# Input projection of a hybrid attention block: three weight tiles over all tokens instead of six over half

## The chip, the cores and the metric

One core of a Trainium2 chip runs the whole program. The metric is the device time of one execution in microseconds; the median of three runs of the kernel before is 1149.23 us (1146.63 to 1149.85).

## The reference

`reference.py` is a two-layer hybrid diffusion backbone on 1024 latent tokens of 1024 channels, with 256 context tokens, all in float32. Only the start of the first (even) layer matters here:

```
shift, scale, gate = silu(c) @ ada_w + ada_b          # 1024 values each
h = layer_norm(x) * (1 + scale) + shift               # 1024 tokens x 1024 channels
z = h @ w_in                                          # split into q, k, v, gates, latent ranks, ...
```

The context tokens go through the same steps with a modulation of their own. After it come gated linear attention and latent attention, an output projection, and a second layer with a Fourier and a spatial gating branch.

## The kernel before

**Number format.** A product of two float32 matrices is made of three TensorE products (`mm3`, L144): each operand is split into a rounded part `hi` (a cast on ScalarE) and the remainder `lo` (a subtraction, mostly on VectorE), and hi x hi, hi x lo and lo x hi are summed in one PSUM bank. There are 8 banks of 128 x 512.

**The start.** `startup` (L275) makes `h` transposed, channels on partitions: for each of 8 channel tiles of 128 a `hi` and a `lo` of 128 x 1024 tokens. A token tile (128 tokens) is loaded and normalized by `load_norm` (L233): statistics on VectorE, three small steps on GpSimd, one activation on ScalarE. TensorE transposes it. Shift and scale of a channel tile come from `modulation` (L243): 512 KB of `ada_w` are loaded and reduced against silu(c) on VectorE, twice per channel tile (custom instruction, L248). So channels "arrive" one by one, with 1 MB each. A weight tile (`weight` in `startup`, L298) is 1024 channels x 128 outputs, 512 KB, rounded on ScalarE (L302), its low part on VectorE or, for two tiles, GpSimd (L305).

There are six weight tiles in `FIRST`: two of q, two of k, and two of latent ranks. The string `ORDER` (L271) sets by hand the order in which steps are written: m is a modulation pair, w a weight, r a channel tile of the first 512 tokens, x a token tile of the second 512, s a channel tile of the second 512, C the state and the context's loads.

The first four token tiles are transposed at once into all 8 banks (L359) and copied from there into `xnT` (L368); GpSimd applies the shift to each of them (L323), ScalarE rounds it (L328), VectorE takes the low part (L329). As each becomes ready, `products` (L342) multiplies it with all weight tiles that are there: six banks hold six tiles x 512 tokens. The second 512 tokens are transposed one channel tile at a time (`second`, L346) in the two other banks, with shift and scale on ScalarE. Then the six banks are evacuated, and `rest` (L398) multiplies the six tiles with the second 512 tokens.

**What follows.** `in_proj_a` (L459) weaves `rest` with the context's own start (`startup_ctx`, L409: 16 reductions, 16 transposes, roundings), in the proportion of the costs that the steps yield, and then projects the 256 context tokens with four of the same weight tiles (96 products of 256 columns). Weights of the two q tiles are given back inside `rest`. Most tiles of 4 KB per partition share one pool of 48 buffers: a load waits in SyncE's queue until a buffer is free.

**Who orders.** A compiler places the instructions of each engine in one fixed list, mostly in the order of the program, but an instruction whose inputs it expects early can be put ahead of others. `k.order(a, b)` (L126) adds a tie without a wait: a stands behind b in the list of their engine. Engines then run their lists strictly in order.

Of the kernel before, what the change touches and what calls it, by code (L numbers as in the profile page):

```python
# [82 lines left out]
class K:  # L83
# [60 lines left out]
    def mm3(self, out, lhs, rhs, start, stop):  # L144
        t = self.nc.tensor
        t.matmul(out, lhs[0], rhs[0], start=start, stop=False)  # L146
        t.matmul(out, lhs[0], rhs[1], start=False, stop=False)  # L147
        t.matmul(out, lhs[1], rhs[0], start=False, stop=stop)  # L148
# [94 lines left out]
def modulation(k, j, which, cB, name, queue, bufs=None):  # L243

    aw = k.b4(name="aw")
    queue.dma_start(aw, k.A["ada0"][which, j])
    o = k.sm.tile([P, 1], F32, tag=f"{name}{which}", name=name, bufs=bufs)
    k.nc.vector.tensor_tensor_reduce(out=aw, in0=aw, in1=cB, scale=1.0, scalar=k.ab[:, j, which:which + 1],  # L248
                                     op0=ALU.mult, op1=ALU.add, accum_out=o)
    return o  # L250
# [20 lines left out]
ORDER = "m w w r m w w r m w r m m x r x x x r m C s r s m s s r s s s s"  # L271
PLO, DVEV, REST_CONSTS = (2, 4), (2, 4), T_KR


def startup(k, context):  # L275
# [9 lines left out]
    xs = [load_norm(k, A["x"][i * P:(i + 1) * P, :]) for i in range(4)]  # L285

    nc.vector.tensor_scalar(out=k.ab[:, :, 1], in0=k.ab[:, :, 1], scalar1=1.0, scalar2=None, op0=ALU.add)
    tiles, ws, mods = FIRST, [], []
    h = ([], [])

# [7 lines left out]
    def weight():  # L298
        n = len(ws)
        raw, hi, lo = k.b4(F32, (P, KD, P), name="wraw"), k.b4(F32R, (P, KD, P), name="hi"), k.b4(F32R, (P, KD, P), name="lo")  # L300
        nc.sync.dma_start(raw, A["we"][tiles[n]])
        nc.scalar.copy(out=hi, in_=raw)  # L302
        ws.append((hi, lo))
        eng = nc.gpsimd if n in PLO else nc.vector
        eng.tensor_tensor(out=lo, in0=raw, in1=f32(hi), op=ALU.subtract)  # L305
        catch_up()
        for j in range(len(h[0])):
            products(n, j)

    def mod():  # L310
        j = len(mods)
        mods.append([])
        for w in range(2):
            mods[j].append(modulation(k, j, w, cB, f"mod{j}", nc.sync, 1))
            catch_up()

    def affine(out, in_, j):

        sh, sc = mods[j]
        if out is not in_:  # L320
            nc.scalar.activation(out=out, in_=in_, func=AF.Identity, scale=sc, bias=sh)
        else:
            nc.gpsimd.tensor_scalar(out=out, in0=in_, scalar1=sc, scalar2=sh, op0=ALU.mult, op1=ALU.add)  # L323

    def part(j, x, o):

        hi, lo = h[0][j][:, o:o + 512], h[1][j][:, o:o + 512]
        nc.scalar.copy(out=hi, in_=x)  # L328
        sub = lambda: nc.vector.tensor_tensor(out=lo, in0=x, in1=f32(hi), op=ALU.subtract)  # L329
        if o:  # L330
            later.append(sub)
            return
        sub()
        for t in range(len(ws) if acc else 0):
            products(t, j)

    def ready(j, x):
        for z in h:
            z.append(k.b4(F32R, name="h"))
        part(j, x, 0)  # L340

    def products(t, j):  # L342
        cnt[t] += 1
        k.mm3(acc[t], (ws[t][0][:, j, :], ws[t][1][:, j, :]), (h[0][j][:, :512], h[1][j][:, :512]), cnt[t] == 1, cnt[t] == KD)

    def second(j):  # L346

        ps = k.bank()
        for i in range(4):
            nc.tensor.transpose(ps[:, i * P:(i + 1) * P], xs[i][:, j * P:(j + 1) * P], k.ident)  # L350
        t = k.w2(name="x2")
        affine(t, ps, j)
        part(j, t, 512)

    cnt, acc = [0] * len(tiles), []
    mod()
    weight()
    ps = [k.bank() for _ in range(KD)]
    for i in range(4):  # L359
        for j in range(KD):  # L360
            nc.tensor.transpose(ps[j][:, i * P:(i + 1) * P], xs[i][:, j * P:(j + 1) * P], k.ident)
    x = k.w2(name="x2")
    affine(x, ps[0], 0)
    ready(0, x)
    xnT = [k.b4(F32, (P, 2, 512), name="xnT") for _ in range(KD // 2)]
    for j in range(1, KD):
# [1242 lines left out]
```

## Time and profile before

| | |
|---|---|
| median of three runs | 1149.23 us |
| profiled execution | 1150.0 us, of it span 1147.5 us |
| TensorE busy | 1091.7 us (95%) |
| VectorE, ScalarE, GpSimd busy | 739.0, 556.6, 260.1 us |
| mean granted TensorE clock | 0.985 of full |
| moved by DMA | 131.89 MB, 115 GB/s over the span |

Busy time is the sum of an engine's instructions. A busy TensorE is not one at its peak, since its matmuls overlap. The granted clock is 1.0 at 2.4 GHz and 0.5 at 1.2 GHz. A timeline row gives start, duration, engine, line, operation, output and inputs with their shapes, and the count of merged instructions; in brackets the idle time before it and what ended it. A windows row gives the busy time of every engine in one stretch.

### The profile page before, as it was taken

To read this page: it belongs to the slowest core of one execution; us is meant where nothing else is said; L and a number is where in the kernel's file an instruction comes from. 1 tells how busy PE (TensorE), PEld (TensorE's weight loads), DVE (VectorE), ACT (ScalarE), POOL (GpSimd) and SP (SyncE) were. 2 spreads that over 40 slices of the span, in tenths; PEclk is the share of its full clock that TensorE was granted. 3 is DMA by queue.
4 is the path that set the end of the run, shared out by engine and by line. 5 is a ranking of instruction groups with operands and counts; after the bars stand their busy time and mean duration, and the time that the engine had idled before them with its cause. 6 is when DMAs were issued, how large, how long until landed. Compare 5 with 4: busy or idle time off the path is not lost.

```text
span 1147.5 us, 14546 instructions
## 1 busy us (share of the span) xinstructions
PE 1091.7 (95%) x5288; PEld 864.4 (75%) x5288; DVE 739.0 (64%) x1256; ACT 556.6 (49%) x956; POOL 260.1 (23%) x260
## 2 busy tenths in 40 slices
PE   5889999899999999999999999999999999999997
PEld 3668778677777777767677666888788888888885
DVE  6867784756655675765778677788526533664544
ACT  6285755576553367857767778313422223332000
POOL 3520000000000023332424466343101000022111
PEclk8989999899999999999999999999999999999999
DMA  9635662333435752113202424323400311125111
GB/s 373 243 127 194 210 229 101 118 119 111 183 120 178 240 156 52 24 47 88 66 4 51 124 74 137 121 110 134 160 1 1 109 38 56 55 69 200 62 55 55
DMA packets 41752, 131.89 MB, mean 115 GB/s; under 512 B 5673, under 2 KB 7465, under 8 KB 41682
## 3 DMA queue, kind: packets, MB, share of 16 engines
q1 hardware_dynamic: 35578, 114.77, 30.5%
q0 software_dynamic: 3312, 10.26, 2.3%
q10 hardware_dynamic: 2792, 5.94, 1.3%
q8 instruction: 41, 0.67, 0.2%
q14 instruction: 29, 0.24, 0.1%
HBM read 98.37 MB, written 20.36 MB: 103 GB/s over the span
## 4 chain that ended last, share of the span: by engine, by line
PE 75%; DVE 8%; ACT 7%; issue 4%; POOL 3%; DMA 3%; SPq 1%; POOLq 0%; DVEq 0%; ACTq 0%
PE ps L146 10%; PE ps L147 10%; PE ps L148 10%; PE pso L146 5%; PE pso L147 5%; PE pso L148 5%; PE pss L1068 3%; PE psm L993 3%; PE pss L1069 3%; PE pss L1070 3%; PE psav L1054 3%; PE psav L1053 2%; PE psav L1052 2%; PE psn L146 1%; PE psn L147 1%
## 5 line engine op out<-in xcount | busy, mean ns | idle before, releaser
L141 POOL TENSOR_TENSOR ph<-pexp,ph 128x512 fp32r<-128x512 f32 x80 | 108.2, 1357 | 167.8 <-ACT ph L136 145.3
L118 ACT ACTIVATE pexp<-pss 128x512 f32<-128x512 f32 x160 | 93.2, 596 | 61.1 <-PE pss L1070 59.4
L146 PE MATMUL ps<-h,hi 128*128 128x512 f32 x256 | 103.8, 417 | 7.4 <-ACT h L328 3.3
L994 DVE TENSOR_REDUCE mx<-psm 128x1 f32<-128x512 f32 (+1 forms) x192 | 102.5, 592 | 10.7 <-PE psm L993 10.3
L148 PE MATMUL ps<-h,lo 128*128 128x512 f32 x256 | 102.6, 401 | 2.8 <-DVE lo L305 1.5
L147 PE MATMUL ps<-h,hi 128*128 128x512 f32 x256 | 104.2, 407 | 0.8 <-DVE h L329 0.8
L141 DVE TENSOR_TENSOR ph<-pexp,ph 128x512 fp32r<-128x512 f32 x80 | 75.1, 943 | 44.6 <-ACT ph L136 42.9
L141 DVE TENSOR_TENSOR lo<-wraw,hi 128x1024 fp32r<-128x1024 f32 x37 | 47.1, 1283 | 85.0 <-ACT hi L136 80.0
L146 PE MATMUL pso<-hi,yh 128*128 128x512 f32 x256 | 99.8, 390 | 0.0
L147 PE MATMUL pso<-lo,yh 128*128 128x512 f32 x256 | 99.7, 390 | 0.0
L148 PE MATMUL pso<-hi,yl 128*128 128x512 f32 x256 | 99.0, 389 | 0.0
L136 ACT CAST ph<-pexp 128x512 fp32r<-128x512 f32 x160 | 95.2, 620 | 2.8
L146 PE MATMUL ps<-h1h,hi 128*128 128x512 f32 x192 | 75.2, 391 | 0.0
L147 PE MATMUL ps<-h1l,hi 128*128 128x512 f32 x192 | 74.7, 389 | 0.0
L148 PE MATMUL ps<-h1h,lo 128*128 128x512 f32 x192 | 74.7, 389 | 0.0
L1135 POOL TENSOR_TENSOR owr<-owr,rowB 128x1024 f32<-128x1024 f32 x16 | 42.8, 2684 | 119.7 <-DMA owr<-wo 119.6
L1054 PE MATMUL psav<-ph,V 128*96 128x512 f32 x160 | 64.0, 400 | 2.5 <-POOL ph L141 2.2
L146 PEld LDWEIGHTS ps<-h,hi 128*128 128x128 f32 x256 | 49.2, 194 | 20.4 <-ACT h L328 4.8
L1052 PE MATMUL psav<-ph,V 128*96 128x512 f32 x160 | 63.2, 395 | 0.2
L148 PEld LDWEIGHTS ps<-h,lo 128*128 128x128 f32 x256 | 49.1, 192 | 16.7 <-DVE lo L305 2.6
L147 PEld LDWEIGHTS ps<-h,hi 128*128 128x128 f32 x256 | 49.4, 193 | 11.3 <-issue 1.7
L148 PEld LDWEIGHTS pso<-hi,yl 128*128 128x128 f32 x256 | 48.1, 188 | 10.1
(359 smaller groups left out, 2590.9 us busy)
## 6 DMA issues: line engine op xcount, KB each, us to landing
aw<-ada SPq DMA_DIRECT2D x32, 512.0 KB, 7.4
araw<-ada SPq DMA_DIRECT2D x32, 512.0 KB, 4.9
wraw<-we SPq DMA_DIRECT2D x16, 512.0 KB, 6.0
owr<-wo SPq DMA_DIRECT2D x16, 512.0 KB, 4.6
xr<-x SPq DMA_DIRECT2D x16, 512.0 KB, 6.9
wraw<-wd SPq DMA_DIRECT2D x12, 512.0 KB, 3.5
xt<-x SPq DMA_DIRECT2D x8, 512.0 KB, 6.0
kt<-kn SPq DMA_DIRECT2D x16, 256.0 KB, 3.6
```

Source lines behind the costliest of these rows:

```text
L118: r = self.nc.scalar.activation(out=out, in_=in_, func=func, **kw)
L136: self.nc.scalar.copy(out=hi, in_=src)
L141: (lo_eng or self.nc.vector).tensor_tensor(out=lo, in0=src, in1=f32(hi), op=ALU.subtract)
L146: t.matmul(out, lhs[0], rhs[0], start=start, stop=False)
L147: t.matmul(out, lhs[0], rhs[1], start=False, stop=False)
L148: t.matmul(out, lhs[1], rhs[0], start=False, stop=stop)
L993: T.matmul(ps[:, :n], q[0][0:96, i * P:(i + 1) * P], cols(kt[0], s, n)[0:96], start=True, stop=True)
L994: nc.vector.reduce_max(out=mx[:, i, b:b + 1], in_=ps[:, :n], axis=AX.X)
L1052: T.matmul(a[0:96, :], vhi(j, hd), hi, start=j == 0, stop=False)
L1054: T.matmul(a[0:96, :], vhi(j, hd), lo, start=False, stop=j == NK - 1)
L1068: T.matmul(ps, kc[0], q[0][:, o], start=True, stop=False)
L1135: k.nc.gpsimd.tensor_tensor(out=raw, in0=raw, in1=k.ogate, op=ALU.mult)
```

## The change

All eight token tiles are loaded near the start: four ahead of the first modulation, four behind the second. Work goes by blocks of one channel tile x 512 tokens (`BLOCKS`): the first two channel tiles' first halves, then their second halves, then both halves of each further tile. `transposed` (t) makes four transposes into a bank, `channels` (r) shifts on ScalarE straight out of the bank and rounds, `low` takes the low part on VectorE, and `products` multiplies the block with the three held weight tiles (`HELD`): six banks now hold three tiles x 1024 tokens, two take transposes. Ties: the transposes of a block stand behind the last product that was written before them, and products stand behind the newest transposes, which are those of the next block; a shift stands behind the newest weight rounding and the rounding of the block before; reductions from the fifth channel on stand behind the newest low part. All low parts of weights are on VectorE. The other three weight tiles are loaded between the later channels and multiplied with all tokens in `rest`. The held banks are evacuated and the context's loads are written behind the last block; the two q tiles' weights are given back there.

```diff
@@ -143,9 +143,9 @@
 
     def mm3(self, out, lhs, rhs, start, stop):
         t = self.nc.tensor
-        t.matmul(out, lhs[0], rhs[0], start=start, stop=False)
+        i = t.matmul(out, lhs[0], rhs[0], start=start, stop=False)
         t.matmul(out, lhs[0], rhs[1], start=False, stop=False)
-        t.matmul(out, lhs[1], rhs[0], start=False, stop=stop)
+        return i, t.matmul(out, lhs[1], rhs[0], start=False, stop=stop)
 
 
     def weight(self, src, shape, hi_eng="act", lo_eng=None):
@@ -240,13 +240,15 @@
     return xt
 
 
-def modulation(k, j, which, cB, name, queue, bufs=None):
+def modulation(k, j, which, cB, name, queue, bufs=None, behind=None):
 
     aw = k.b4(name="aw")
     queue.dma_start(aw, k.A["ada0"][which, j])
     o = k.sm.tile([P, 1], F32, tag=f"{name}{which}", name=name, bufs=bufs)
-    k.nc.vector.tensor_tensor_reduce(out=aw, in0=aw, in1=cB, scale=1.0, scalar=k.ab[:, j, which:which + 1],
-                                     op0=ALU.mult, op1=ALU.add, accum_out=o)
+    r = k.nc.vector.tensor_tensor_reduce(out=aw, in0=aw, in1=cB, scale=1.0, scalar=k.ab[:, j, which:which + 1],
+                                         op0=ALU.mult, op1=ALU.add, accum_out=o)
+    if behind:
+        k.order(r, behind)
     return o
 
 
@@ -268,8 +270,9 @@
 FIRST = (T_GQ, T_GQ + 1, T_GK, T_GK + 1, T_KR, T_CKV)
 
 
-ORDER = "m w w r m w w r m w r m m x r x x x r m C s r s m s s r s s s s"
-PLO, DVEV, REST_CONSTS = (2, 4), (2, 4), T_KR
+ORDER = ("x x x x m w t r w t m r x x x x t r t m w r " + 2 * "t m r t r " + 3 * "t m w r t r " + "t r t r")
+BLOCKS = [(0, 0), (1, 0), (0, 512), (1, 512)] + [(j, o) for j in range(2, KD) for o in (0, 512)]
+HELD, REST_CONSTS = 3, T_KR
 
 
 def startup(k, context):
@@ -282,12 +285,11 @@
     k.sc, k.ab = small[:, 0:8], small[:, 8:24].rearrange("p (j w) -> p j w", w=2)
     k.m12, k.mlow = small[:, 24:88], small[:, 88:152].bitcast(I32)
     k.gng, k.mlag = small[:, 152:153], small[:, 153:156]
-    xs = [load_norm(k, A["x"][i * P:(i + 1) * P, :]) for i in range(4)]
+    k.act(k.sc, k.sc, AF.Silu)
 
     nc.vector.tensor_scalar(out=k.ab[:, :, 1], in0=k.ab[:, :, 1], scalar1=1.0, scalar2=None, op0=ALU.add)
-    tiles, ws, mods = FIRST, [], []
+    tiles, ws, mods, xs, there, cast = FIRST, [], [], [], [], []
     h = ([], [])
-
 
     later = []
 
@@ -296,112 +298,100 @@
             later.pop(0)()
 
     def weight():
-        n = len(ws)
+        n = len(cast)
         raw, hi, lo = k.b4(F32, (P, KD, P), name="wraw"), k.b4(F32R, (P, KD, P), name="hi"), k.b4(F32R, (P, KD, P), name="lo")
         nc.sync.dma_start(raw, A["we"][tiles[n]])
-        nc.scalar.copy(out=hi, in_=raw)
-        ws.append((hi, lo))
-        eng = nc.gpsimd if n in PLO else nc.vector
-        eng.tensor_tensor(out=lo, in0=raw, in1=f32(hi), op=ALU.subtract)
-        catch_up()
-        for j in range(len(h[0])):
-            products(n, j)
+        cast.append(nc.scalar.copy(out=hi, in_=raw))
+
+        def low():
+            nc.vector.tensor_tensor(out=lo, in0=raw, in1=f32(hi), op=ALU.subtract)
+            ws.append((hi, lo))
+            for b in there if n < HELD else ():
+                products(n, *b)
+
+        later.append(low)
 
     def mod():
         j = len(mods)
         mods.append([])
         for w in range(2):
-            mods[j].append(modulation(k, j, w, cB, f"mod{j}", nc.sync, 1))
+            mods[j].append(modulation(k, j, w, cB, f"mod{j}", nc.sync, 1, lows[-1] if j > 3 else None))
             catch_up()
 
...
+    turned, todo, lows, turns, behind, rounded = [], list(BLOCKS), [], [], [], []
+
+    def transposed():
+        j, o = todo.pop(0)
         ps = k.bank()
         for i in range(4):
-            nc.tensor.transpose(ps[:, i * P:(i + 1) * P], xs[i][:, j * P:(j + 1) * P], k.ident)
...
+            turn = nc.tensor.transpose(ps[:, i * P:(i + 1) * P], xs[o // P + i][:, j * P:(j + 1) * P], k.ident)
+            if i == 0 and behind:
+                k.order(turn, behind[0])
+        turned.append((j, o, ps))
+        turns.append(turn)
+
+    def channels():
+
+        j, o, ps = turned.pop(0)
+        if not o:
+            for z in h:
+                z.append(k.b4(F32R, name="h"))
+        sh, sc = mods[j]
+        x = k.w2(name="x2")
+        hi, lo = h[0][j][:, o:o + 512], h[1][j][:, o:o + 512]
+
+        i = nc.scalar.activation(out=x, in_=ps, func=AF.Identity, scale=sc, bias=sh)
+        k.order(i, cast[-1])
+        if rounded:
+            k.order(i, rounded[-1])
+        rounded.append(nc.scalar.copy(out=hi, in_=x))
+
+        def low():
+            lows.append(nc.vector.tensor_tensor(out=lo, in0=x, in1=f32(hi), op=ALU.subtract))
+            there.append((j, o))
+            for n in range(min(len(ws), HELD)):
+                products(n, j, o)
+
+        later.append(low)
+
+    cnt, acc = {}, {}
+
+    def products(n, j, o):
+        if (n, o) not in acc:
+            acc[n, o], cnt[n, o] = k.bank(), 0
+        cnt[n, o] += 1
+        i, last = k.mm3(acc[n, o], (ws[n][0][:, j, :], ws[n][1][:, j, :]), (h[0][j][:, o:o + 512], h[1][j][:, o:o + 512]),
+                        cnt[n, o] == 1, cnt[n, o] == KD)
+        behind[:] = [last]
+
+        k.order(i, turns[-1])
+
+    do = {"w": weight, "m": mod, "t": transposed, "r": channels}
     for e in ORDER.split():
-        if e == "w":
-            weight()
-        elif e == "m":
-            mod()
-        elif e == "r":
-            j = len(h[0])
-            x = xnT[j // 2][:, j % 2, :]
-            affine(x, x, j)
-            ready(j, x)
-        elif e == "x":
-            i = 4 + len(xs)
-            xs.append(load_norm(k, A["x"][i * P:(i + 1) * P, :]))
+        if e == "x":
+            xs.append(load_norm(k, A["x"][len(xs) * P:(len(xs) + 1) * P, :]))
             catch_up()
...
+            if e in "rw":
+                catch_up()
+            do[e]()
     catch_up()
-    for n, t in enumerate(tiles):
-        evac[t](acc[n], 0)
+    assert len(there) == 2 * KD and all(c == KD for c in cnt.values()) and len(ws) == len(tiles)
+    del xs[:]
+    evac = even_state(k)
+    for n in range(HELD):
+        for o in (0, 512):
+            evac[tiles[n]](acc[n, o], o)
+    next(context)
     k.keep = dict(zip(tiles, ws))
+    for t in (T_GQ, T_GQ + 1):
+        del k.keep[t]
 
     def rest():
-        for t in tiles:
+        for t in tiles[HELD:]:
             if t == REST_CONSTS:
                 gla_consts(k)
-            yield from k.proj_steps(k.keep[t], h, evac[t], first=512)
-            if t in (T_GQ, T_GQ + 1):
-                del k.keep[t]
+            yield from k.proj_steps(k.keep[t], h, evac[t])
 
     return h, rest()
```

## Rows read from the trace of the kernel before

**Rows 1.** The page: TensorE's busy tenths in 40 slices of 28.7 us.

```profile
PE   5889999899999999999999999999999999999997
```

**Rows 2.** Windows: length, busy us (instructions) of five engines, clock, DMA share, GB/s.

```profile
18.00:40.00 22.00, 15.80 (x47) 10.19 (x47) 18.06 (x21) 9.46 (x14) 9.64 (x5) 0.77 1.03 408
40.00:56.00 16.00, 14.84 (x65) 11.74 (x65) 14.53 (x27) 3.74 (x5) 8.63 (x12) 1.00 0.41 155
56.00:66.00 10.00, 6.59 (x26) 5.17 (x27) 3.65 (x8) 9.18 (x13) 1.93 (x5) 0.66 0.00 0
66.00:75.60 9.60, 7.77 (x38) 5.96 (x36) 6.38 (x13) 7.57 (x11) 5.07 (x7) 1.00 0.49 174
75.60:111.00 35.40, 35.37 (x163) 28.85 (x164) 26.79 (x44) 24.59 (x44) 1.57 (x3) 1.00 0.55 182
111.00:124.00 13.00, 13.00 (x106) 12.73 (x105) 10.16 (x18) 5.31 (x12) 1.39 (x2) 1.00 0.72 251
```

**Rows 3.** Timeline, TensorE: start us, us, line, operation, tiles, shape, count.

```profile
28.17 0.63 PE L146 MATMUL ps<-h,hi 128*128 128x512 f32 x1
...
30.30 0.63 PE L147 MATMUL ps<-h,hi 128*128 128x512 f32 x1
...
41.10 0.40 PE L146 MATMUL ps<-h,hi 128*128 128x512 f32 x1
...
45.64 0.39 PE L148 MATMUL ps<-h,lo 128*128 128x512 f32 x1
...
68.82 1.03 PE L350 MATMUL ps<-ident,xt 128*128 128x128 f32 x8
```

**Rows 4.** Timeline, ScalarE, 14 to 18 us.

```profile
14.56 1.24 ACT L239 ACTIVATE xt<-xt,nm,rstd 128x1024 f32<-128x1024 f32 x1 [2.04 <-POOL nm L214]
16.22 0.78 ACT L321 ACTIVATE x<-ps,mod,mod 128x512 f32<-128x512 f32 x1 [0.42 <-PE ps L361]
16.90 1.03 ACT L302 CAST hi<-wraw 128x1024 fp32r<-128x1024 f32 x1
17.83 0.62 ACT L328 CAST h<-x 128x512 fp32r<-128x512 f32 x1
```

**Rows 5.** Timeline, VectorE: first reductions, and the last context low part.

```profile
9.85 1.23 DVE L207 BATCH_NORM_STATS2 bnst<-xt 128x6 f32<-128x512 f32 x2
...
11.25 1.29 DVE L248 CUSTOM_DVE_ANT_0 aw<-aw,cB,small 128x1024 f32<-128x1024 f32 x1
...
12.46 1.28 DVE L248 CUSTOM_DVE_ANT_0 aw<-aw,cB,small 128x1024 f32<-128x1024 f32 x1
...
17.96 1.23 DVE L305 TENSOR_TENSOR lo<-wraw,hi 128x1024 fp32r<-128x1024 f32 x1 [4.21 <-ACT hi L302]
19.11 0.68 DVE L329 TENSOR_TENSOR h<-x,h 128x512 fp32r<-128x512 f32 x1
...
120.42 0.42 DVE L141 TENSOR_TENSOR clo<-ct,chi 128x256 fp32r<-128x256 f32 x1
```

**Rows 6.** Timeline, GpSimd: the small steps of the second and fourth token tile.

```profile
8.62 0.23 POOL L198 TENSOR_SCALAR rstd<-bnmv 128x1 f32<-128x1 f32 x1
...
9.60 0.27 POOL L214 TENSOR_SCALAR nm<-bnmv,rstd 128x1 f32<-128x1 f32 x1
...
11.41 1.21 POOL L198 TENSOR_SCALAR rstd<-bnmv 128x1 f32<-128x1 f32 x1 [0.16 <-DVE bnmv L209]
...
14.26 0.26 POOL L214 TENSOR_SCALAR nm<-bnmv,rstd 128x1 f32<-128x1 f32 x1
```

**Rows 7.** Windows of 10 us, columns as in rows 2.

```profile
0.00:10.00 10.00, 3.97 (x5) 1.36 (x6) 4.75 (x15) 4.95 (x7) 2.80 (x12) 1.00 0.78 286
10.00:20.00 10.00, 6.35 (x34) 5.56 (x34) 5.75 (x10) 7.40 (x10) 3.98 (x6) 1.00 1.03 420
```

**Rows 8.** Windows of 2 us, columns as in rows 2.

```profile
62.00:64.00 2.00, 1.60 (x8) 1.50 (x8) 0.92 (x2) 2.00 (x4) 0.00 (x0) 0.50 0.00 0
...
66.00:68.00 2.00, 2.00 (x11) 1.63 (x10) 2.00 (x6) 1.98 (x4) 0.80 (x3) 1.00 0.00 0
```

More of the change, by code (lines that the diff above doesn't have):

```diff
@@ L313, in mod @@
         for w in range(2):
-            mods[j].append(modulation(k, j, w, cB, f"mod{j}", nc.sync, 1))
+            mods[j].append(modulation(k, j, w, cB, f"mod{j}", nc.sync, 1, lows[-1] if j > 3 else None))
             catch_up()
[L317 to L344, printed above, removed]
@@ L346, in second @@
-    def second(j):
+    turned, todo, lows, turns, behind, rounded = [], list(BLOCKS), [], [], [], []
+    def transposed():
+        j, o = todo.pop(0)
         ps = k.bank()
         for i in range(4):
-            nc.tensor.transpose(ps[:, i * P:(i + 1) * P], xs[i][:, j * P:(j + 1) * P], k.ident)
[L351 to L355, printed above, removed]
-    mod()
-    weight()
[L358 to L366, printed above, removed]
-        cp = nc.vector.tensor_copy if j in DVEV else nc.scalar.copy
-        cp(out=xnT[j // 2][:, j % 2, :], in_=ps[j])
-    k.act(k.sc, k.sc, AF.Silu)
-    acc += [k.bank() for _ in tiles]
-    products(0, 0)
-    xs, sec = [], iter(range(KD))
-    evac = None
-    for e in ORDER.split():
-        if e == "w":
-            weight()
-        elif e == "m":
-            mod()
-        elif e == "r":
-            j = len(h[0])
-            x = xnT[j // 2][:, j % 2, :]
-            affine(x, x, j)
-            ready(j, x)
-        elif e == "x":
-            i = 4 + len(xs)
-            xs.append(load_norm(k, A["x"][i * P:(i + 1) * P, :]))
+            turn = nc.tensor.transpose(ps[:, i * P:(i + 1) * P], xs[o // P + i][:, j * P:(j + 1) * P], k.ident)
@@ L387, in startup @@
             catch_up()
-        elif e == "s":
-            second(next(sec))
-        else:
-            evac = even_state(k)
-            next(context)
+        else:
+            if e in "rw":
+                catch_up()
+            do[e]()
     catch_up()
-    for n, t in enumerate(tiles):
-        evac[t](acc[n], 0)
+    assert len(there) == 2 * KD and all(c == KD for c in cnt.values()) and len(ws) == len(tiles)
[4 more added lines that the diff above has]
+            evac[tiles[n]](acc[n, o], o)
```

## The prediction

> **What bounds the kernel now.** I read the page's slices first: TensorE is busy nine tenths or more nearly everywhere and leaves room only at the front [rows 1]. So the change is worth what the first 125 us are worth, and I cut these with the view of busy time by stretch [rows 2]. From 75.6 us on TensorE has no gap (35.37 of 35.40 us, then 13.00 of 13.00). Before that it has: 15.80 of 22 us at a mean clock of 0.77 from 18 to 40 us, 14.84 of 16, then 6.59 of 10 at 0.66, and 7.77 of 9.6. In 56 to 66 us the DMA share is 0.00: that hole is no wait for data from memory. It is the second half of the tokens, normalized and transposed late, with ScalarE at 9.18 of 10 us.
>
> What is left at 75.6 us is pure TensorE work. The stretch holds 163 of its instructions, 16 of them context transposes, so about 147 products of the six input tiles. There are 6 tiles x 8 channels x 2 halves x 3 = 288 such products in all, before and after. The changed kernel leaves 3 tiles x 48 = 144 to the part behind the arrival. So it stands where the old one stood at 75.6 us, plus 3 products of 0.23 us, when its three held tiles are finished: **the gain is 76.3 us minus that moment**, if the part behind runs as densely as now.
>
> **The change part by part.** First the price of the pieces. A product at full clock: 20 starts from 41.10 to 45.64 us, 0.227 us each; at half clock five in 2.13 us, 0.426 each; eight transposes in 1.03 us, 0.13 each [rows 3]. ScalarE: normalizing a token tile 1.24 us, the shift and scale 0.78, rounding a channel block 0.62, rounding a weight tile 1.03 [rows 4]. VectorE, start to start: statistics of a token tile 1.40 (9.85 to 11.25), one modulation reduction 1.21, the low part of a weight 1.2, the low part of a block 0.68 [rows 5].
>
> Removed: seven evacuations into xnT, seven GpSimd shifts, two low parts of weights on GpSimd. Added: seven blocks' shift on ScalarE and two low parts on VectorE. Over the arrival ScalarE then has 16 x 1.40 + 6 x 1.03 + 8 x 1.24 = 38.5 us and VectorE 8 x 1.40 + 16 x 1.21 + 6 x 1.2 + 16 x 0.68 = 48.6 us, both under the time at hand. TensorE has 144 x 0.227 + 64 x 0.13 = 41.0 us. Per block of 512 tokens that is 9 x 0.227 + 4 x 0.13 = 2.57 us. With the transposes one block ahead, shift, rounding and low part (0.78 + 0.62 + 0.68 = 2.08) run under 2.05 us of products and the next 0.5 us of transposes. VectorE needs per channel two reductions, two low parts and, three times, a weight's: 3.8 to 5.0 us against 5.14. So **once the fourth block flows, TensorE sets the pace**, and what counts is when the blocks of the second token half start: they need all eight token tiles, and by the new ties every later transpose stands behind them.
>
> That start, in the order in which the code gives VectorE its work. The four first tiles end as now, the last normalized at 15.8 us [rows 4]. The first weight's rounding, which now must precede the shift: 16.85. Shift 17.6, rounding 18.25, low part 18.9. Then VectorE: reduction 20.1, low part of weight two 21.3, reduction 22.5. Only now can channel 1 be shifted (23.3) and rounded (23.9), while VectorE takes the statistics of the fifth tile (23.9). Low part of channel 1, 24.6; three more tiles at 1.40, 28.8. The last tile's GpSimd steps take 1.25 us undisturbed (8.62 to 9.87) and 3.1 us beside two modulation reductions (11.41 to 14.52) [rows 6]; here one reduction follows, so I take the middle, 2.2: 31.0. Normalizing: 32.3. Memory is not late for this: in the new order the eighth token tile is the 14th transfer of 0.52 MB, 7.4 MB in all, and 7.1 MB had moved by 20 us [rows 7], so it lands near 21 us.
>
> From 32.4 us TensorE has 56 transposes and 144 - 12 = 132 products left, 7.3 + 30.0 = 37.3 us. Filling the chain costs the first block's shift, rounding and low part, 2.1 us, less the 0.5 us of the next block's transposes: 1.6. TensorE will have idled before, and the clock restarts at half. In the old kernel it was at 0.50 through 62 to 64 us and 1.00 from 66 on [rows 8]; some 3 us of work at half speed lose 1.5 us. Done at 32.4 + 37.3 + 1.6 + 1.5 = **72.8 us, 3.5 us earlier than 76.3**.
>
> The Trainium skill ("TensorE: Matmul & The Clock Gate", Part 4: PE-mode transpose) says that transposes do not register as TensorE activity for the clock as products do. The row of 62 to 64 us agrees: 1.60 of 2 us busy, nearly all transposes, clock still 0.50. By that rule a phase with a fifth of its time in transposes could be held at half clock; it is the last rival below.
>
> Behind the arrival: six held banks are evacuated in 18 ScalarE copies and 6 on VectorE instead of the 11 and 12 of the old first halves, while TensorE goes on with the fourth tile in the two banks that the transposes leave. Six banks are full at that moment, but the next one is wanted only 48 products, 11 us, later. The context work (16 reductions of 1.21 us and its small steps) has to end before TensorE has done 144 products, 16 transposes and 96 context products, some 46 us; the last context low part of the old kernel ended at 120.8 us, 45 us after 75.6 [rows 5]. The new order frees four weight buffers at the start of this stretch rather than within it, and adds 7 ScalarE copies to its head. I count zero for it, with -1 to +3.5 us as bounds: a bit earlier data, or the whole gain lost in waiting for the context.
>
> **Sum.** The profiled execution takes 1150.0 us with a span of 1147.5; minus 3.5 is 1146.5. The median of the runs is 1149.23, 0.8 lower, so I forecast **1145.7 us**, with 1143 to 1148 for this case. Its softest term is the 32.4 us.
>
> **Rivals.** A: the compiler's ordering puts the late token tiles ahead. For: they have landed by 21 us, and VectorE is idle before the first low part (12.46 + 1.2 to 17.96 [rows 5]). Against: the old queue left that same gap open. The VectorE work that must precede is 11.2 us from 11.3 us on (four reductions, two weights' and two blocks' low parts, four statistics, 14 us with the gap filled): 25.4, plus 1.25 and 1.24 is 28 us, 4.4 earlier: 1141.3.
>
> B: the gain is made and given back. The context channels, not TensorE, end the stretch, since their chain runs through ScalarE copies that queue behind the evacuations: 1149.2. For it: the old chain's last low part came 45 us into those 46. Against: its 16 reductions are 19.4 us of them, so most of the chain is waiting that can shift.
>
> C, slower: VectorE's order during the arrival. Only the reductions from the fifth channel on are tied behind a low part; the context's reductions are free, can be loaded once the last weight is in, and stand in the same queue. Place: between a block's rounding and its low part. TensorE stalls from the point where more than 2.57 - 0.68 = 1.9 us of other work stands between two low parts. Price: two statistics and five reductions, 2.8 + 6.05 = 8.9 us, less some 3 us that VectorE has spare over channels 2 to 4, is a 6 us stall: +2.5 us net, 1151.7. With weights' low parts also falling there, 1154.
>
> D: the clock stays at half through the arrival: 132 products x 0.2 us = 26 us more, 1172. Against it: from 66 to 68 us, with products again, the clock was back at 1.00 [rows 8].
>
> **Chances.** Forecast 0.40, A 0.24, B 0.16, C 0.17, D 0.03. Leaving out D, the far end of C and gains beyond A's, the range is 1139 to 1153. About 0.3% (3.4 us) is what a measurement of this kernel can tell from no change. The forecast lies on that line: half of it counts as faster, with A and a little more 0.45; the other half and B, less what of B ends above the line, 0.35; C and D 0.20.
>
> **What would show it.** The first transpose of the second token half between 31 and 34 us; from about 38 us TensorE with under 0.3 us idle per block, each 2.57 us long; the three held tiles done near 73 us; the last context product near 120 rather than 123 us; from there all stages 3.5 us earlier. Wrong if the low part waits behind reductions (C), if the fifth tile's statistics stand ahead of channel 1's reductions (A), or if TensorE waits for context data at the end of the stretch (B).

## The result, and the profile after

The changed kernel takes 1162.45 us (median of four runs, 1160.83 to 1168.21) where the kernel before took 1147.93 us beside it (four runs, 1145.66 to 1149.85): ratio 1.0133, 95% interval 1.0101 to 1.0164. It is slower by some 15 us; forecast was 1145.7 us. The profiled execution of after is the longest of its four (1168.21 us, span 1166.4), so only its start is read closely here.

Windows of the kernel after, columns as in [rows 2]; the first four have the same bounds as there.

```profile
18.00:40.00 22.00, 11.32 (x30) 6.70 (x31) 15.24 (x27) 11.24 (x13) 5.94 (x12) 0.69 1.03 420
40.00:56.00 16.00, 16.00 (x75) 13.07 (x74) 9.82 (x16) 7.96 (x11) 0.95 (x1) 0.89 0.13 44
56.00:66.00 10.00, 8.88 (x48) 7.15 (x47) 8.23 (x13) 6.16 (x9) 0.00 (x0) 1.00 0.00 1
66.00:75.60 9.60, 8.47 (x43) 6.78 (x42) 5.13 (x8) 4.83 (x7) 0.00 (x0) 1.00 0.75 257
75.60:84.00 8.40, 8.40 (x38) 6.66 (x38) 3.45 (x5) 7.11 (x14) 0.00 (x0) 1.00 0.85 309
84.00:98.00 14.00, 6.65 (x19) 4.63 (x18) 9.06 (x16) 10.54 (x15) 4.23 (x7) 0.64 0.18 56
98.00:124.00 26.00, 26.00 (x120) 21.24 (x120) 19.25 (x34) 10.68 (x20) 1.75 (x3) 1.00 0.54 186
124.00:136.00 12.00, 12.00 (x99) 11.87 (x98) 6.92 (x12) 4.40 (x10) 0.00 (x0) 1.00 0.56 178
```

The arrival, from the first loads to the last product of the held tiles, idles less from 56 us on (8.88 and 8.47 us busy, against 6.59 and 7.77 in [rows 2]). But TensorE is busy only 11.32 us from 18 to 40 us (15.80 before), and a new hole stands at 84 to 98 us, with the granted clock at 0.64 there. The timeline of TensorE in the kernel after shows the steps:

```profile
35.52 0.69 PE L327 MATMUL ps<-ident,xt 128*128 128x128 f32 x2 [2.52 <-ACT xt L239]
37.51 1.22 PE L146 MATMUL ps<-h,hi 128*128 128x512 f32 x2 [1.30 <-ACT h L347]
...
43.81 0.60 PE L327 MATMUL ps<-ident,xt 128*128 128x128 f32 x4
46.33 0.60 PE L327 MATMUL ps<-ident,xt 128*128 128x128 f32 x4
...
58.34 0.50 PE L147 MATMUL ps<-h,hi 128*128 128x512 f32 x1 [1.12 <-DVE h L350]
...
69.80 0.50 PE L147 MATMUL ps<-h,hi 128*128 128x512 f32 x1 [1.13 <-DVE h L350]
...
74.28 0.60 PE L327 MATMUL ps<-ident,xt 128*128 128x128 f32 x4
...
84.17 0.39 PE L148 MATMUL ps<-h,lo 128*128 128x512 f32 x1
91.40 0.69 PE L413 MATMUL ps<-ident,xt 128*128 128x128 f32 x2 [6.84 <-ACT xt L239]
```

The last token tile reaches TensorE at 35.5 us. Blocks then follow 2.52 us apart, with two stalls of 1.1 us behind a block's low part. 18 products remain after the last token transposes of 74.28, so the held tiles end at 74.64 + 18 x 0.227 = 78.7 us. TensorE then does one half tile ahead of the context and stands 6.84 us for the context's normalized rows. ScalarE of the kernel after says why: they stand in its list behind the copies of the held tiles.

```profile
78.41 9.30 ACT L507 ACTIVATE dup<-ps 64x512 f32<-64x512 f32 x16 [1.20 <-DVE dup L509]
87.74 1.06 ACT L118 ACTIVATE ccB<-ccB 128x1024 f32<-128x1024 f32 x1
88.81 1.28 ACT L114 ACT_TABLE_LOAD   x1
90.11 1.24 ACT L239 ACTIVATE xt<-xt,nm,rstd 128x1024 f32<-128x1024 f32 x1
92.58 1.24 ACT L239 ACTIVATE xt<-xt,nm,rstd 128x1024 f32<-128x1024 f32 x1 [1.24 <-POOL nm L214]
```

The kernel before did the same norm inside the arrival, where TensorE was waiting anyway (its ScalarE timeline):

```profile
68.77 1.24 ACT L239 ACTIVATE xt<-xt,nm,rstd 128x1024 f32<-128x1024 f32 x1 [0.78 <-POOL nm L214]
...
71.89 1.25 ACT L239 ACTIVATE xt<-xt,nm,rstd 128x1024 f32<-128x1024 f32 x1 [1.22 <-POOL nm L214]
```

I use one landmark below, the **context's end**: the start of ScalarE's copy of the last context bank (tile wzst, 32 x 256). It is 122.43 us before and 135.87 after:

```profile
122.43 0.37 ACT L175 CAST wzst<-ps 32x256 fp32r<-32x256 f32 x1 [2.29 <-PE ps L148]
135.87 0.37 ACT L175 CAST wzst<-ps 32x256 fp32r<-32x256 f32 x1 [4.09 <-PE ps L148]
```

The 13.4 us between them are 2.4 us of arrival (78.7 against 76.3), 6.8 + 0.5 us of waiting for the norm, and some 3 us of products at half clock behind it (0.43 us apart until 98 us); 0.7 us is left over. That sum shows where TensorE stood idle, not what would have come of it otherwise; the runs tell that.

### The profile page after: what moved, and what is told of

Same layout as the page of the kernel before. It is cut to its first block, busy times and chain, and to the rows that moved or that the text cites. A ratio compares the mean times of both kernels' runs of the same rounds, so it can differ in the third digit from the quotient of the medians.

```text
span 1166.4 us, 14548 instructions
## 1 busy us (share of the span) xinstructions
PE 1097.2 (94%) x5288; PEld 867.9 (74%) x5288; DVE 741.8 (64%) x1256; ACT 561.2 (48%) x958; POOL 245.9 (21%) x251
## 4 chain that ended last, share of the span: by engine, by line
PE 76%; DVE 9%; ACT 6%; issue 3%; DMA 3%; POOL 2%; SPq 1%; POOLq 0%; DVEq 0%; ACTq 0%
PE ps L146 11%; PE ps L147 11%; PE ps L148 11%; PE pso L148 5%; PE pso L146 5%; PE pso L147 5%; PE psm L983 3%; PE pss L1058 3%; PE pss L1059 2%; PE pss L1060 2%; PE psav L1044 2%; PE psav L1042 2%; PE psav L1043 2%; PE psn L146 1%; PE psn L148 1%
## 5 line engine op out<-in xcount | busy, mean ns | idle before, releaser
L146 PE MATMUL ps<-h,hi 128*128 128x512 f32 x256 | 107.4, 425 | 6.9 <-ACT h L347 5.1
L984 DVE TENSOR_REDUCE mx<-psm 128x1 f32<-128x512 f32 (+1 forms) x192 | 102.5, 595 | 10.2 <-PE psm L983 9.9
L147 PE MATMUL ps<-h,hi 128*128 128x512 f32 x256 | 105.4, 412 | 2.5 <-DVE h L350 2.5
L198 POOL TENSOR_SCALAR rstd<-bnmv 128x1 f32<-128x1 f32 x34 | 24.6, 723 | 172.7 <-DVE bnmv L1160 110.2
```

Source lines behind the costliest of these rows:

```text
L146: i = t.matmul(out, lhs[0], rhs[0], start=start, stop=False)
L984: nc.vector.reduce_max(out=mx[:, i, b:b + 1], in_=ps[:, :n], axis=AX.X)
```

## The experiments

Two theories. **One**: each piece of idle TensorE counts for its own length, the hole most. **Two**: behind the arrival the context's chain (VectorE reductions, ScalarE shift and rounding, VectorE low part, eight channels) ends the stretch whatever TensorE does meanwhile; then only what moves that chain's start or pace counts. Each run of an experiment is timed in five rounds against the kernel before on the same chip; the chips differ between runs, so runs are compared by their ratios. The context's end is read from one execution of each.

| run | made from | ratio to before, 95% interval | context's end, us |
|---|---|---|---|
| after | | 1.0133 [1.0101, 1.0164] | 135.87 |
| e1_context_first | after | 1.0115 [1.0095, 1.0135] | 131.49 |
| e2_context_later | after | 1.0140 [1.0117, 1.0162] | 134.78 |
| e3_low_behind | after | 1.0080 [1.0061, 1.0098] | 130.70 |
| e4_tiles_early | after | 1.0089 [1.0070, 1.0107] | 130.80 |
| e11_after_norm_moved | after | 1.0134 [1.0107, 1.0162] | 132.96 |
| e5_three_together | e1 + e3 + e4 | 1.0046 [1.0026, 1.0066] | 125.70 |
| e7_half_reductions | e5 | 1.0005 [0.9986, 1.0024] | 119.04 |
| b1_before_half_reductions | before | 1.0004 [0.9984, 1.0024] | 122.37 |
| e6_context_faster | e5 | 1.0028 [1.0009, 1.0047] | 124.90 |
| e8_context_two_first | e6 | 1.0016 [0.9996, 1.0036] | 125.06 |
| e9_norm_in_arrival | e8 | 1.0019 [1.0005, 1.0033] | 124.91 |
| e10_in_turn | e9 | 1.0049 [1.0029, 1.0068] | 125.71 |
| e12_balanced_act | e9 | 1.0014 [0.9997, 1.0030] | 123.03 |
| e13_even_copies | e12 | 1.0038 [1.0020, 1.0055] | 127.05 |
| e14_channel_between | e13 | 1.0046 [1.0027, 1.0065] | 125.39 |
| e15_stats_spread | e12 | 1.0094 [1.0077, 1.0112] | 133.60 |
| e16_two_channels | e15 | 1.0128 [1.0105, 1.0150] | 134.56 |
| e17_lows_on_vector | e12 | 0.9992 [0.9975, 1.0009] | 120.54 |

**The hole.** e1 hands the context's loads and norm out ahead of the held tiles' copies, e2 one half tile later, e11 takes the loads and the norm into the arrival (the silu stays where it was).

```diff
+    next(context)            # e1: ahead of the loop over evac[...]
...
-    run(weave((first, FIRST_T), (context, CTX_T)))
+    run(weave((first, FIRST_T), (chain(lull(4.5), context), CTX_T)))   # e2
...
-3 * "t m w r t r " + "t r t r"
+3 * "t m w r t r " + "c t r c t r"     # e11: c normalizes one context tile
```

> The context's start (its loads, silu, the normalizing of its two token tiles) is written ahead of the evacuation of the six held banks instead of behind it; nothing else moves. Theory 1: the loss sits in one hole behind the arrival, 6.8 us in which TensorE's list waits at the context's first transposes for ScalarE, which first makes 18 evacuation copies (78.4 to 87.7 us), a silu and a table load, plus some 3 us because the clock restarts at half. Then the hole shrinks to under 2 us and the time falls by 7 to 10 us, to 1152 to 1155. Theory 2: the chain of the context as a whole is too long for the 46 us behind the arrival, wherever it stands; then the wait moves to the context's last products and the time falls by 3 us at most.

> ScalarE's program order stays as in the changed kernel; only the weave starts the context's steps after about a quarter of the remaining products, so that some 32 products stand ahead of the first context transposes in TensorE's list. Theory 1: the hole is filled by these products and the time falls by 7 to 10 us as in the run before. Theory 2: the context, started 7 us later still, ends later, TensorE waits for it at its end, and the time stays or rises by up to 7 us.

> The changed kernel with one part undone: the context's two tiles are loaded and normalized between its last blocks instead of behind the arrival; its order of blocks and its evacuation are as they are. Theory 1 (the hole behind the arrival costs its length): 6.8 us of hole and 3 us of half clock behind it go, less 2 to 3 us for later low parts: about 1155 us. Theory 2 (the context's chain ends the stretch whatever TensorE does meanwhile): the first reductions still stand behind the held copies on VectorE and start at 86 to 88 us instead of 89.3: 1160 to 1163 us, with TensorE waiting for ct at the context's end.

In e1 the hole is gone and TensorE is fully busy from 77.6 to 110 us; in e11 0.5 us of it is left, in e2 4.0 us. None of the three is faster than the change by what the times can tell. Windows of e1, then its waits of 66 to 136 us (microseconds in total, times, longest):

```profile
84.00:98.00 14.00, 14.00 (x65) 11.43 (x65) 5.20 (x9) 10.07 (x18) 0.00 (x0) 1.00 0.21 56
98.00:110.00 12.00, 12.00 (x56) 9.83 (x55) 9.78 (x17) 6.58 (x13) 0.08 (x1) 1.00 0.40 132
110.00:132.00 22.00, 17.05 (x115) 14.76 (x114) 17.46 (x30) 7.55 (x16) 1.67 (x3) 1.00 0.69 245
```

```profile
PE ps L146 <- ACT ct L415: 3.2, 3, 1.8
```

Much of what TensorE saved it loses again: 5 us idle from 110 to 132 us, most of it waiting for the context's shift (ct). Theory one's 7 to 10 us did not come. In e11 the first reduction even starts later, 93.18 us against 89.28, since the context's silu stayed behind ScalarE's copies.

The traces do give the hole a price, a smaller one. The last token transposes of e1 to e5, in this order, start here:

```profile
73.34 0.60 PE L327 MATMUL ps<-ident,xt 128*128 128x128 f32 x4
72.92 0.60 PE L327 MATMUL ps<-ident,xt 128*128 128x128 f32 x4
70.61 0.60 PE L327 MATMUL ps<-ident,xt 128*128 128x128 f32 x4
69.72 0.60 PE L327 MATMUL ps<-ident,xt 128*128 128x128 f32 x4
67.52 0.60 PE L327 MATMUL ps<-ident,xt 128*128 128x128 f32 x4
```

From there to the context's end pass 60.1 to 61.9 us where the hole stands (after, e2, e3, e4) and 58.2 us where it is closed (e1, e5). So the hole costs some 3 us, by one execution of each, too few for the times to tell, and not the 10 us of idling and half clock. In the kernel after, TensorE has no gap from 98 to 136 us: there it still ends the stretch itself, late by the hole. Once the hole is closed, it waits for the context.

**The arrival.** e3 puts a weight's low part behind the block's, so that no more than two reductions stand between two low parts; e4 takes the statistics of the last four token tiles ahead of channels 1 to 3.

```diff
-3 * "t m w r t r "
+3 * "t m r t w r "                                      # e3
...
-"x x x x m w t r w t m r x x x x t r t m w r "
+"x x x x m w x x x x t r w t m r t r t m w r "          # e4
```

> In the last three channels a weight's step stands one place later, so that on VectorE one reduction, a block's low part, the other reduction and the weight's low part follow each other instead of both reductions and the weight's low part between two blocks' low parts. The two stalls of 1.1 us at 56.7 and 68.2 us go. Theory 1, and the claim that every microsecond of the arrival passes through: 2.2 us faster. Theory 2 (the context ends the stretch): no change.

> The second four token tiles are loaded behind the first weight and ahead of the second weight and the second modulation, so that their statistics stand ahead of channel 1's reductions on VectorE. The transposes of the second token half then start near 26 us instead of 29.4 to 36. If the start of that half sets the arrival (my prediction's softest term), the held tiles are done 6 to 8 us earlier, near 72 us instead of 79, and the time falls as much, to 1154 to 1157, with the hole behind it as before. Rival: VectorE's own sum of work (48 us) or the last channel's data take over, 3 us or less.

The last token transposes start at 70.61 us in e3 and 69.72 in e4 (74.28 after), 3.7 and 4.6 us earlier. Against e1 and e2, whose arrival is written as in after, it is 2.3 to 2.7 and 3.2 to 3.6 us; single executions of one arrival differ by that much. The ratio falls by 0.0053 and 0.0044, 6 and 5 us: e3 by more than either theory had for it (2.2 us or none), e4 by less than the 6 to 8 us of its first theory. The hole is unchanged in both (6.8 us). So lateness in the arrival does count, since TensorE's remaining work and the context's chain both start behind it.

**Which bound.** e5 joins the three edits; e7 and b1 cut the context's reductions in half (half of its modulation sums is left out), in e5 and in the kernel before.

```diff
+    d = D // 2 if name == "modc" else D                 # e7, b1
-    r = ...tensor_tensor_reduce(out=aw, in0=aw, in1=cB, ...
+    r = ...tensor_tensor_reduce(out=aw[:, :d], in0=aw[:, :d], in1=cB[:, :d], ...
```

> The three edits of the first four runs in one kernel: all eight token tiles' statistics ahead of the first weight tile, the last weight tiles' low parts behind a block's low part, and the context's rows normalized ahead of the held tiles' evacuation. Theory 1 (lateness in the arrival and the hole behind it are separate terms, each worth its own length): 4.5 + 3.4 us of the single edits add up and the hole's 6.8 us come on top: about 1147 us. Theory 2 (behind the arrival the context's chain of reductions, not TensorE, sets the end): the earlier arrival counts, the hole does not: 1152 to 1156 us, with TensorE waiting on ScalarE's ct at the end of the context as when the context alone was first.

> The kernel of three edits with the context's sixteen reductions over 512 of the 1024 columns: half of the context's modulation sums is left out, loads and everything else as they are. If VectorE's time in the chain sets the end, 16 x 0.6 us = up to 9.6 us go. If the order in the lists sets it (a step waits for its turn, not for the reduction), under 3 us go.

> A control: the kernel before with the context's sixteen reductions over 512 of 1024 columns (half of the context's modulation sums is left out), the same cut that took 4 us from the changed kernel with three edits. If in the kernel before TensorE ends the stretch (it was busy 100% from 76 to 120 us) and the chain of reductions only keeps up with it, the time stays within 0.3%. If the chain was the bound there too, 3 to 5 us go.

The ratio of e5 is 0.0087 (10 us) below the change's, about the sum of e3 and e4; the times show no gain from closing the hole beside theirs. In the traces the last token transposes come 6.8 us earlier than in after and the context's end 10.2 us; the difference is about the hole's 3 us. The cut takes another 4.0 us (1154.76 to 1150.80; 6.7 us at the context's end) in the changed order and nothing in the old one (0.1 us at the context's end). That is theory two's bound with its control: **once the hole is closed, the context's chain bounds the new order; in the old one TensorE does.** Windows of e5, columns as above:

```profile
74.00:98.00 24.00, 24.00 (x112) 19.66 (x111) 10.86 (x18) 17.15 (x28) 1.96 (x6) 1.00 0.28 93
98.00:110.00 12.00, 11.77 (x65) 9.85 (x64) 11.85 (x21) 4.68 (x9) 1.69 (x3) 1.00 0.50 155
110.00:126.00 16.00, 11.25 (x80) 9.79 (x79) 11.75 (x21) 5.76 (x12) 0.07 (x1) 1.00 0.74 286
```

and of b1:

```profile
75.60:111.00 35.40, 34.98 (x160) 28.54 (x161) 21.14 (x45) 24.99 (x45) 1.57 (x3) 1.00 0.57 196
111.00:124.00 13.00, 13.00 (x105) 12.73 (x104) 7.70 (x18) 5.37 (x12) 1.33 (x2) 1.00 0.70 243
```

Read the third busy time of each row, VectorE. In e5 it works 10.86 of 24 us while ScalarE copies banks, then 11.85 of 12 us, and TensorE begins to wait. Before, the same work was spread, 26.79 of 35.4 and 10.16 of 13 us [rows 2]. It is the same engine with the same reductions; they are handed out too late. In e5 the second channel's first reduction starts 10.6 us behind the first channel's, before 5.1 us (91.69 against 86.58). VectorE of e5:

```profile
82.61 1.27 DVE L248 CUSTOM_DVE_ANT_0 aw<-aw,ccB,small 128x1024 f32<-128x1024 f32 x1
...
93.21 1.27 DVE L248 CUSTOM_DVE_ANT_0 aw<-aw,ccB,small 128x1024 f32<-128x1024 f32 x1
```

In b1 VectorE has 5.65 and 2.46 us less to do there, and TensorE is as busy as before within 0.4 us.

**Order or place.** e6 raises the context's weight in the weave, e8 hands its first channel out ahead of the held copies, e9 brings its norm into the arrival, e10 deals copies, channels and remaining half tiles in turn.

```diff
-CTX_T ... = 19.0
+CTX_T ... = 31.0                        # e6
+    next(context)                       # e8: a second time
+... + "c t r c t r"                     # e9: c as in e11
+    for n in range(HELD):               # e10
+        next(context); evac both banks of n; 4 x next(r) if n < 2
```

> The kernel of three edits, and the weight of the context's stream in the weave raised from 19 to 31, so that nearly two context channels instead of one are given out per half tile: the reductions stand further ahead in VectorE's list and ct, chi further ahead in ScalarE's. If the order of the lists sets the chain's pace, the context projection ends 4 to 10 us earlier than without it and the time falls by as much. If VectorE's or the loads' own time sets it, or the held copies on ScalarE do, the change is under 2 us, or the time rises because evacuations wait behind ct.

> As the kernel with the raised weight, and the context's first channel (two reductions, transposes, ct, chi, clo) ahead of the held tiles' evacuation too. If the chain's start sets its end (reductions began at 88.4 us while VectorE was idle from 80), they begin near 78 us and 3 to 6 us more go. If the held tiles' banks are what TensorE waits for next, the 18 copies on ScalarE start 4 to 6 us later, the first remaining tile waits, and the time is the same or higher.

> As the kernel with the context's first channel ahead of the held evacuation, and the two context tiles loaded and normalized between the last three token blocks (statistics behind a block's low part on VectorE, the norm on ScalarE), as the kernel before had them inside its arrival; only the silu of the context's row stays behind. If the hole of 7 us on TensorE between the last held product and the first context transposes (71 to 78.8 us) is now what sets the end, it closes but for the bank waits and 4 to 6 us go (about 1147 us). If VectorE's chain of reductions still ends last, they begin at about 71 instead of 74 us: 1 to 3 us. If the statistics delay the last two blocks' low parts by their own 2.8 us each, at most half of that remains.

> As the run before, and the held evacuation, the first three context channels and the first two remaining half tiles handed out in turn (channel, two banks, half tile) instead of one channel, six banks, then the rest: the second channel's reductions no longer wait for all six of VectorE's copies (they stood idle or behind copies until 88.9 us). If that wait counts, 2 to 4 us less than the run before; if VectorE's copies keep their place ahead of the reductions, no change within 0.2%.

None of these steps is clear by itself; from e5 to e9 the medians fall by 4 us (1154.76 to 1150.73), with intervals that just overlap. Each moved the wait to the next list: in e6 TensorE waits 3.9 us for a held bank's copy, in e8 4.3 us for the norm, in e9 2.8 us for a copy again. e10 came out 3 us above e9 by the medians, against all that was expected of it; why is open. One cost of e9, e10 and e11 lies in the edit: a step c first writes out what is due, and standing ahead of a t it puts a block's products ahead of the next block's transposes. TensorE then waits for that block's shift and rounding (in e9 1.5 and 0.8 us).

**What is left.** e12 takes work off the two lists: the context's norm and three weights' low parts to GpSimd, the silu ahead of the last pair, all held copies to ScalarE. e13 splits the copies evenly, e14 puts the second channel between them. e15 spreads the context's statistics over four blocks, e16 hands two channels out first. e17 is e12 with the low parts back on VectorE, two of them behind the first context channel.

```diff
-    nc.vector.tensor_tensor(out=lo, in0=raw, ...)
+    eng = nc.vector if n < HELD else nc.gpsimd          # e12
-    if d == hh or s:
+    if d == hh or s or nm == "q":                       # e12; e13: if d == hh:
+    sub() if n <= HELD else late.append(sub)            # e17, on VectorE
```

> The three edits of the arrival, the raised weight and the context's first channel first, and now the work that stood in ScalarE's and VectorE's lists behind the arrival taken off it: the context's two norms run on GpSimd between the last blocks and its silu ahead of the last pair, the low parts of the three weight tiles that are not held run on GpSimd, and all 24 copies of the held tiles on ScalarE. If only lists and engines' places cost the change its gain (TensorE is never idle from the last held product on), the context projection ends near 71.3 + 46.8 = 118 us, where 46.8 us is what the kernel before took from its first remaining product to there, and the time is 1144 to 1146 us, below the kernel before. If ct waits behind the 24 copies (13 us), it ends at 121 to 124 us: 1148 to 1150 us. If GpSimd's additions slow VectorE's two-input work in the arrival, the last block is later and the time stays at 1151 us.

> As the run before with the held tiles' 24 copies split evenly, twelve on ScalarE and twelve on VectorE. If ScalarE's list holds the second channel up, ct comes 6 us earlier and the time is 1 to 3 us lower; if VectorE's reductions do (twelve copies of 0.7 us stand ahead of them), it is 1 to 3 us higher.

> As the run with even copies, and the context's second channel handed out behind the first held tile's copies instead of behind all three: its reductions stand behind six VectorE copies, its ct behind nine of ScalarE's. If the chain still bounds, 1 to 3 us less than with even copies and below the kernel before (1145 to 1147 us); if TensorE is the bound by now, no change.

> As the run with all copies on ScalarE, but the context's tiles are loaded two blocks earlier and their statistics given out in halves of 0.64 us over four blocks instead of 2.8 us at a time: in that run TensorE stood 1.55 + 0.48 us behind low parts delayed by them, and 2.62 us at the context's first transposes behind GpSimd's norm. If those 4.7 us of idle TensorE are on the path, 3 to 5 us go and the time is 1145 to 1147 us, below the kernel before. If the chain of reductions ends the stretch there too (its second channel's reductions began at 89.4 us behind a remaining tile's copies), the time stays at 1150 us.

> As the run before, and the context's second channel too ahead of the held tiles' copies: its reductions follow the first channel's at once (about 76 us instead of 89), its ct stands behind ten copies instead of 25. If the chain bounds, 2 to 4 us less than the run before; if TensorE does, no change or a little more, as the held banks come free later.

> As the run with all copies on ScalarE, but no low part of a weight tile runs on GpSimd: the first of the three stays on VectorE in its place, the two others run there behind the context's first channel, in VectorE's idle time (77.8 to 88 us in that run). There one reduction took 3.42 instead of 1.28 us while GpSimd took a low part, and the context's second norm waited 2.4 us behind another. If these two stalls of TensorE (1.55 and 2.62 us) are on the path, 3 to 4 us go: about 1146 us, below the kernel before by 0.2 to 0.3%. If something else ends the stretch, the time stays at 1150 us; if the third tile's low part in its old place delays the blocks as before, 1148 us.

e12 came 5 us later to the context's end than the 118 us worked out for it: TensorE lost 1.55 us in the arrival to a reduction that ran beside GpSimd (last section) and 2.62 us to the norm behind another low part there. e13 and e14 reached the context's end 4 and 2.4 us later than e12; TensorE stood 1.6 and 1.0 us for ct in them, and the rest of that is open. e15 and e16 failed for a reason outside both theories, the same cost of the edit: c now stands right behind an r in most places, so that in six places the products written ahead leave TensorE nothing to do while the next block is shifted and rounded. The last token transposes start at 81.01 us in e15 and at 68.67 in e12. The trace has six such waits, the first of the two rows (waits of e15, 36 to 90 us):

```profile
PE ps L146 <- ACT h L364: 6.9, 6, 1.5
PE ps L147 <- DVE h L367: 3.0, 2, 1.8
```

e17 removes e12's stall in the arrival and all but 0.8 us of the one at the norm. Its windows:

```profile
72.00:110.00 38.00, 37.71 (x170) 30.66 (x169) 23.54 (x38) 24.99 (x45) 1.06 (x2) 0.98 0.51 178
110.00:120.60 10.60, 10.60 (x86) 10.38 (x85) 10.45 (x20) 4.90 (x10) 0.52 (x1) 1.00 0.51 157
```

TensorE is busy 48.31 of 48.6 us there, and the context ends at 120.54 us, 1.9 us ahead of the kernel before. At 1148.64 against 1149.92 us it is level with it; whether it is faster is not settled.

## Why the prediction was wrong

- **The start at 32.4 us, called its softest term: 3.1 us too early.** VectorE, kernel after:

```profile
24.46 0.69 DVE L350 TENSOR_TENSOR h<-x,h 128x512 fp32r<-128x512 f32 x1 [1.55 <-ACT h L347]
25.07 1.28 DVE L207 BATCH_NORM_STATS2 bnst<-xt 128x6 f32<-128x512 f32 x2
...
30.97 1.23 DVE L248 CUSTOM_DVE_ANT_0 aw<-aw,cB,small 128x1024 f32<-128x1024 f32 x1
...
32.12 1.28 DVE L248 CUSTOM_DVE_ANT_0 aw<-aw,cB,small 128x1024 f32<-128x1024 f32 x1
```

  All four statistics stand behind channel 1's low part, none in the gap of 1.55 us ahead of it, and take 1.47 us each: they end at 31.05 us, not 28.8. Two reductions follow, not one, and the last tile's GpSimd steps take 3.1 us as in the slow case of [rows 6], not 2.2. Rival A, the compiler filling that gap, did not happen; done by hand (e4) it gave 3.2 to 4.6 us at the last transposes, near A's 4.4. (A's 25.4 us is 11.3 + 14; its "11.2 us" does not fit the list behind it.)
- **37.3 us of work, 1.6 of filling, 1.5 of clock:** 43.2 us passed from 35.5 to 78.7, 2.8 more than counted. The clock is one part: products stood at half clock from 37.51 to 43.8 us, 15 of them, which lost some 2.9 us and not 1.5. The two stalls are the other, 2.25 us; the filling and the shorter blocks give the rest back. The period per block was right (2.52 for 2.57 us). That TensorE idles under 0.3 us per block held but for two blocks. There rival C's condition held, more than 1.9 us of other work between two low parts, though with two of the arrival's own reductions and a weight's low part and not with the context's; it cost 1.12 and 1.13 us instead of C's 6:

```profile
53.45 0.69 DVE L350 TENSOR_TENSOR h<-x,h 128x512 fp32r<-128x512 f32 x1 [1.31 <-ACT h L347]
54.06 1.28 DVE L248 CUSTOM_DVE_ANT_0 aw<-aw,cB,small 128x1024 f32<-128x1024 f32 x1
...
56.47 1.22 DVE L307 TENSOR_TENSOR lo<-wraw,hi 128x1024 fp32r<-128x1024 f32 x1
57.61 0.68 DVE L350 TENSOR_TENSOR h<-x,h 128x512 fp32r<-128x512 f32 x1
```

  The count of VectorE's time per channel (up to 5.0 us against 5.14) was not what failed; that this work must also fall evenly between the low parts stood in rival C alone and was not priced in the forecast.
- **Zero behind the arrival, bounds -1 to +3.5 us: the step that failed most.** From the held tiles' end to the context's end 57.2 us passed where the forecast had 46.1 (122.43 less its break-even of 76.3): 11 us lost, where it counted none. I had counted the context's steps as unmoved, but the change moved its loads (on SyncE's queue from 34 to 68 us), its norm and its silu from the arrival's idle time to behind the held copies. The prediction listed what was removed and added on each engine, not the steps that only changed their place. Of the 11 us, closing the hole gives back some 3 (e1, e5). Behind that the chain of reductions sets the end: halving them in e5 gives back 6.7 us at the context's end, and nothing in the kernel before. Rival B named the right mechanism, ScalarE's copies ahead of the context's chain, but bounded its price by the gain; the chain's delay has no such bound.
- **Half clock through the arrival (D)** did not come: with four transposes to nine products per block the granted clock was 1.00 from 56 to 84 us. The Trainium skill's rule ("TensorE: Matmul & The Clock Gate", Part 4: PE-mode transpose), that transposes do not count as busy in the way products do, is neither shown nor refuted by that, as products fill four fifths of each block.

From the change to e17 the ratio falls by 0.0141, 16 us: 10 us up to e5, by the arrival and the hole, some 3 by the context's first steps (e6 to e9), and some 3 by e12 and e17. The forecast's 3.5 us of gain were not reached by any run. Its break-even of 76.3 us assumed that the stretch behind runs as densely as before, and in the changed kernel it did not.

## What to carry to other kernels

An idle stretch of the busiest engine can be where another stage's preparation is hidden, as the context's was here; before filling it, list what runs there on every other engine and say where each goes. Closing a wait on the trace gains less than its length if a chain on another engine ends the stretch soon behind it (here some 3 of 10 us). To find such a chain, halve that chain's work in both kernels: the one that gets faster is bound by it. An engine's busy share over a whole stage hides this; look at whether it is idle early and full late.

## What the runs showed of the hardware

**VectorE and GpSimd block each other.** In e12 one reduction with two inputs in the on-chip buffer took 3.42 instead of 1.28 us beside GpSimd's low part (3.40 in e13, 3.42 in e14). VectorE, then GpSimd:

```profile
56.56 1.28 DVE L251 CUSTOM_DVE_ANT_0 aw<-aw,cB,small 128x1024 f32<-128x1024 f32 x1
...
57.76 3.42 DVE L251 CUSTOM_DVE_ANT_0 aw<-aw,cB,small 128x1024 f32<-128x1024 f32 x1
```

```profile
51.91 2.44 POOL L311 TENSOR_TENSOR lo<-wraw,hi 128x1024 fp32r<-128x1024 f32 x1 [26.60 <-ACT hi L307]
56.95 3.15 POOL L311 TENSOR_TENSOR lo<-wraw,hi 128x1024 fp32r<-128x1024 f32 x1 [2.60 <-ACT hi L307]
```

GpSimd's second low part takes 0.7 us more than its first, about the time to the end of VectorE's first reduction at 57.8; VectorE's second reduction ends 1.1 us behind GpSimd's end at 60.1. So each seems to have waited for the end of the other's instruction. The Trainium skill ("SBUF — State Buffer", Who interferes with whom) says that a VectorE instruction with two inputs in that buffer contends with a GpSimd instruction that reads it, and calls the ports that they share "an exclusive lock"; these rows agree.

**The clock behind a hole.** After 6.84 us without work TensorE took up at half clock, 0.43 us per product from 91.7 to 98 us, and the window of 98 to 124 us shows 1.00. Where e1 closed the hole the clock stayed at 1.00 (its window of 84 to 98 us); the time did not change by what can be told.
